# A recurrence's first step and the preparation of its second half, both ten half tiles later in the emission order

## The chip, the cores and the metric

One core of one Trainium2 chip runs the whole program. The metric is the device time of one execution in microseconds (us). The kernel before takes 2046.28 us, the median of three runs (2044.22 to 2046.51).

## The reference

A model with two blocks over 512 tokens of width 1024, all in float32. The first block has two layers. Each projects the modulated and normalised input `h` with one wide matrix, gives the pieces to three mixers (a causal pool mixer, a retention with 4 heads, an RWKV-7 time mix with 8 heads), gates the three results, merges them and projects back. The second block is attention and a mixture of 32 experts; the change does not touch it. The part that matters here is the time mix, in the reference a scan over the tokens:

```python
def step(S, inp):
    r_t, w_t, k_t, v_t, a_t, b_t = inp
    sa = jnp.einsum('bhvk,bhk->bhv', S, a_t)
    S = (S * w_t[:, :, None, :] + sa[..., None] * b_t[:, :, None, :]
         + v_t[..., None] * k_t[:, :, None, :])
    return S, jnp.einsum('bhvk,bhk->bhv', S, r_t)
```

## The kernel before

**Dense tiles.** The projections are cut into tiles of 128 output columns by 512 tokens. A tile is 24 matmuls of 128x512: 8 blocks of the inner width, each as three products of high and low parts (`mm3`, L313; the matmul itself is L354 without and L356 with a pin, see below). Its weights come by SyncE's queue (SP) into one of three buffers (`wst`, L297), ScalarE takes the high part (L307) and VectorE, or GpSimd for one tile in five, the low part (L310).

**Side work in half tiles.** After every half tile, `mm3` calls `tick` (L363), which takes generators of side work one step further: the recurrence (`rwkv`, L507), the retention's heads (`ret_heads`, L1045) and the pool mixer's groups (`pool_groups`, L931). With `RWKV_RATE = 1.0` the recurrence goes one `yield` per half tile. What they emit goes between the dense matmuls.

**Order on the engines.** A planner makes one fixed list for each engine before the program runs, by the order of emission and by its own costs of what is ready. On the chip each engine goes through its list in order. One thing is written by hand: each step of the recurrence sets `self.pin`, and `mm3` puts the next dense tile's first matmul behind that pin (`pinned`, L358). Dense work emitted after a step of the recurrence can therefore not run ahead of that step.

**The recurrence of a layer** goes over chunks of 64 tokens in two halves of four heads. `rwkv_prep` (L559, 19 yields) prepares a half: norms and decays (L571 to L628), the Gram matrices (L646, stored by L650), and then the inverses by forward substitution, 31 steps of two VectorE instructions each (L674 a product, L676 a sum), each needing the one before. Its result goes to memory (L682, L684). `rwkv_chain` (L688) is the recurrence itself: after `wait` empty yields it loads the first chunks' Gram matrices and inverses (`gt` L698, `ti` L700), and its first step is `inverse1`, whose matmul reads `ti`, then four steps per chunk. `rwkv` runs the preparation of the first half, then the chain of the first half beside the preparation of the second (through `late`, L515), then the chain of the second half, then the outputs (`rwkv_out`, L846).

**What runs beside it.** In half tiles from the start of the side work: 0 to 8 the retention's values, 8 to 20 the six tiles of the second half's r, k and v, 20 to 36 the eight q and k tiles of the retention, each turned by a rotary embedding (VectorE L1024, L1026 and L1027, then an add on GpSimd, L1028), 36 to 52 the pool mixer's eight tiles, 52 to 76 the first branch (gate tiles and branch tiles), 76 to 124 the second branch and the gates ahead of the third. At 124 `self.drain(rs)` (L1126) takes what is left of the recurrence. The first preparation ends at half tile 20, the first step of the chain comes at 26, and the second preparation begins at 21, since its tiles are there only then.

Of the kernel before, what the change touches and what calls it, by code (L numbers as in the profile page):

```python
# [179 lines left out]
class Layers:  # L180
# [326 lines left out]
    def rwkv(self, l, t, wa, out):  # L507
        prep = lambda hf: self.rwkv_prep(l, hf, t[hf][0:2], t[hf][2:4], t[hf][4:6], wa)
        ops = yield from prep(0)
        ys, nxt = yield from self.both(self.rwkv_chain(l, *ops, wait=CHAIN_WAIT), self.late(t, prep))  # L510
        (_, ys) = yield from self.both(self.rwkv_out(0, ys, ops[3]), self.rwkv_chain(l, *nxt))
        yield from self.rwkv_out(1, ys, nxt[3])
        out += ops[3] + nxt[3]

    def late(self, t, prep):  # L515
        while len(t) < 2:
            yield
        return (yield from prep(1))
# [1424 lines left out]
ATT_RATE = 4.0  # L1943
NEX = 5
NOH = 3
CHAIN_WAIT = 6


# [14 lines left out]
```

## Time and profile before

| | us |
|---|---|
| median of three runs | 2046.28 |
| the profiled execution | 2044.99 |
| its span, first to last instruction | 2043.2 |
| TensorE busy with matmuls | 1862.0 (91%) |
| VectorE busy | 1088.7 (53%) |
| ScalarE busy | 591.8 (29%) |
| GpSimd busy | 549.4 (27%) |
| mean granted TensorE clock, share of 2.4 GHz | 0.946 |

The first layer lies at about 60 to 740 us, the second at 740 to 1440 us, the second block behind them. A matmul's row overlaps the next one's, since matmuls are pipelined, so the distance between starts is what a matmul costs in a run of them. Of the 40 slices of the span (51 us each) TensorE is busy under 70% in four: the first, the fifth (204 to 255 us, 40 to 49%), the eighteenth (868 to 919 us, 60 to 69%) and the last. The fifth and the eighteenth lie one in each layer, at the same place of its work.

### The profile page before, as it was taken

The page shows a single profiled execution, that of the slowest core. Times are in us where ns is not written, and L with a number is a line of the kernel's source. Part 1 is how long each engine was busy: PE and PEld are TensorE (multiplying, and loading weights), DVE is VectorE, ACT ScalarE, POOL GpSimd, SP SyncE. Part 2 cuts the span into 40 slices and gives each one's busy share as a digit, 9 for nine tenths or more (in the row PEclk, how much of TensorE's full clock was granted, in tenths as well). Part 3 has the DMA queues.
Part 4 walks back from the last instruction along what each step waited for, and adds up shares of the span by engine and source line. Part 5 has one row for each costly group of instructions (what it writes and reads, how often), then busy time and mean ns, then how long its engine had stood idle before and what let it go on. Part 6 is the DMA issues. An engine that isn't in the chain of part 4 may idle for free. (4 is left out here: it accounts for less than half of the span.)

```text
span 2043.2 us, 26468 instructions
## 1 busy us (share of the span) xinstructions
PE 1862.0 (91%) x10178; PEld 1364.9 (67%) x10178; DVE 1088.7 (53%) x2285; ACT 591.8 (29%) x1086; POOL 549.4 (27%) x447
## 2 busy tenths in 40 slices
PE   6899498999999989967999999999999999899996
PEld 3777266777787868745667778777778768444443
DVE  4656779644533555495774243246554546344435
ACT  3332112332322333221233232234334334111112
POOL 1342244454566401232330122230110122100000
PEclk9999598999999989978899999999999969899998
DMA  7424143333343533312322323243422225799981
GB/s 296 134 90 117 30 119 87 97 122 118 108 145 108 172 102 93 119 47 60 109 67 88 92 66 93 83 118 118 168 73 78 73 109 217 312 424 416 403 347 42
DMA packets 103128, 289.03 MB, mean 141 GB/s; under 512 B 31112, under 2 KB 44296, under 8 KB 94808
## 3 DMA queue, kind: packets, MB, share of 16 engines
q1 hardware_dynamic: 97912, 267.40, 38.4%
q0 software_dynamic: 5088, 19.93, 2.6%
q8 instruction: 81, 1.33, 0.3%
q14 instruction: 47, 0.39, 0.1%
HBM read 268.90 MB, written 21.01 MB: 142 GB/s over the span
## 5 line engine op out<-in xcount | busy, mean ns | idle before, releaser
L354 PE MATMUL mm<-hi,wlo 128*128 128x512 f32 x1424 | 567.5, 399 | 2.0 <-DVE wlo L310 1.5
L354 PE MATMUL mm<-lo,whi 128*128 128x512 f32 x1424 | 567.0, 398 | 0.1
L354 PE MATMUL mm<-hi,whi 128*128 128x512 f32 x1296 | 519.3, 401 | 15.3 <-DVE rw L502 6.2
L307 ACT ACTIVATE whi<-wst 128x1024 fp32r<-128x1024 f32 (+1 forms) x202 | 193.0, 957 | 575.7 <-PE mm L354 390.1
L354 PEld LDWEIGHTS mm<-hi,wlo 128*128 128x128 f32 x1424 | 272.2, 191 | 69.6 <-issue 4.5
L354 PEld LDWEIGHTS mm<-lo,whi 128*128 128x128 f32 x1424 | 273.0, 192 | 63.7 <-issue 6.5
L354 PEld LDWEIGHTS mm<-hi,whi 128*128 128x128 f32 x1296 | 248.0, 192 | 77.8 <-ACT hi L486 7.8
L310 DVE TENSOR_TENSOR wlo<-wst,whi 128x1024 fp32r<-128x1024 f32 (+1 forms) x162 | 188.0, 1162 | 180.6 <-ACT whi L307 169.3
L310 POOL TENSOR_TENSOR wlo<-wst,whi 128x1024 fp32r<-128x1024 f32 (+1 forms) x40 | 87.5, 2188 | 279.7 <-ACT whi L307 279.6
L1802 PE MATMUL pp<-eg,xt 128*64 128x512 f32 x512 | 114.8, 601 | 0.2 <-PEq L1852 0.2
L437 POOL TENSOR_TENSOR wad<-wad,cact 128x1024 f32<-128x1024 f32 x32 | 65.3, 2040 | 180.2 <-DMA wad<-wada 150.7
L439 POOL TENSOR_TENSOR wad<-wad 128x512 f32<-128x512 f32 (+2 forms) x96 | 98.0, 1021 | 6.2
L1802 PEld LDWEIGHTS pp<-eg,xt 128*64 128x64 f32 x512 | 37.2, 139 | 74.7 <-issue 74.4
L354 PE MATMUL mm<-vhi,hi 128*128 128x256 f32 x256 | 75.3, 298 | 6.2 <-ACT vhi L970 4.0
L908 POOL TENSOR_TENSOR acc<-acc,tg 128x512 f32<-128x512 f32 x32 | 49.9, 1561 | 97.3 <-DVE tg L906 80.2
L354 PE MATMUL mm<-vlo,hi 128*128 128x256 f32 x256 | 74.9, 295 | 0.7 <-DVE vlo L971 0.6
L354 PE MATMUL mm<-vhi,lo 128*128 128x256 f32 x256 | 74.4, 292 | 0.0
L1842 PE MATMUL mm<-y,ohT 128*128 128x512 f32 x256 | 69.2, 409 | 3.2 <-DVE xr L1844 1.6
L1770 POOL DMA_INDIRECT xg<-hx,idx x16 | 15.5, 969 | 205.7 <-DVE xt L1793 151.0
L356 PE MATMUL mm<-hi,whi 128*128 128x512 f32 x128 | 65.5, 511 | 0.0
L674 DVE TENSOR_TENSOR tmp<-tt,lt 64x31 f32<-64x31 f32 (+15 forms) x124 | 58.2, 469 | 9.8 <-DMA lt<-gd 7.9
L1827 PE MATMUL ms<-ed,eht 128*64 128x512 f32 x256 | 58.7, 599 | 4.2 <-ACT eht L1817 4.0
(408 smaller groups left out, 2863.6 us busy)
## 6 DMA issues: line engine op xcount, KB each, us to landing
wst<-win SPq DMA_DIRECT2D x154, 512.0 KB, 3.7
eg<-egu SPq DMA_DIRECT2D x31, 2048.0 KB, 14.2
ed<-edn SPq DMA_DIRECT2D x31, 1024.0 KB, 10.2
wad<-wada SPq DMA_DIRECT2D x48, 512.0 KB, 4.2
wst<-wbr SPq DMA_DIRECT2D x48, 256.0 KB, 2.8
gd<-gs SPq DMA_DIRECT2D x64, 128.0 KB, 2.2
gt<-gd SPq DMA_DIRECT2D x32, 256.0 KB, 3.0
wst<-wout SPq DMA_DIRECT2D x16, 512.0 KB, 4.1
```

The costliest lines, as they stand in the source:

```text
L307: nc.scalar.activation(hi, w, AF.Copy)
L310: e.tensor_tensor(lo, w, hi.bitcast(F32), op=OP.subtract)
L354: return op(*args, **kw)
L356: return op(*args, **kw)
L437: nc.gpsimd.tensor_tensor(w, w, self.cact.unsqueeze(2).to_broadcast([128, 8, 128]), op=OP.mult)
L439: nc.gpsimd.tensor_add(w[:, :n], w[:, :n], w[:, n:2 * n])
L674: nc.vector.tensor_tensor(t, tt[:, 0:j + 1, j:j + 1].to_broadcast([2 * nu, j + 1, n]), lt[:, j:j + 1, j + 1:].to_broadcast([2 * nu, j + 1, ...
L908: nc.gpsimd.tensor_add(acc[d], acc[d], t)
L1770: self.last_row = self.nc.gpsimd.indirect_dma_start(xg, None, self.hx[:, :], bass.IndirectOffsetOnAxis(ap=idx, axis=0))
L1802: nc.tensor.matmul(p[64 * i:64 * i + 64], x[:, k, 64 * i:64 * i + 64], wts[e + i][0][:, k], start=k == 0, stop=k == 7)
L1827: nc.tensor.matmul(py[64 * i:64 * i + 64], ht[:, 128 * k + 64 * i:128 * k + 64 * i + 64], wts[e + i][1][:, k, 512 * c:512 * c + 512], star ...
L1842: nc.tensor.matmul(p, oT[:, 128 * tb:128 * tb + 128], y, start=i == 0, stop=i == len(parts) - 1)
```

## The change

Two constants. The chain of the first half waits 16 yields instead of 6 before its first loads, and the preparation of the second half lets 10 yields pass before it looks whether its tiles are there. Both are in each of the two layers.

```diff
     def late(self, t, prep):
+        for _ in range(PREP_WAIT):
+            yield
         while len(t) < 2:
             yield
         return (yield from prep(1))
...
-CHAIN_WAIT = 6
+CHAIN_WAIT = 16
+PREP_WAIT = 10
```

No instruction is added or taken away. In half tiles, the chain's first step goes from 26 to 36; the second preparation goes from 21 to 30, nine later, since one yield passed before with the tiles not there yet. The chain of the first half then ends at 69 instead of 59, that of the second at 103 instead of 93.

## Rows read from the trace of the kernel before

**Rows 1.** Stretches: start:end, length, busy PE, PEld, DVE, ACT, POOL, clock, DMA.

```profile
198.90:246.20 47.30, 14.17 (x46) 7.32 (x44) 37.31 (x71) 7.83 (x12) 15.91 (x13) 0.54 0.16 42
890.40:935.20 44.80, 15.89 (x57) 8.84 (x56) 34.88 (x73) 8.78 (x13) 13.00 (x9) 0.59 0.14 33
246.20:397.00 150.80, 135.89 (x915) 104.11 (x915) 115.85 (x257) 41.57 (x77) 66.03 (x53) 0.93 0.32 92
```

**Rows 2.** Waits of TensorE: waiter, what it waited for: total us, times, longest.

```profile
PE rm L354 <- DMA ti<-tn: 42.3, 2, 22.0
PE pp L356 <- DVE pbd L802: 14.1, 9, 4.4
```

**Rows 3.** Timeline, TensorE around the first step: start, us, engine, line, operation.

```profile
198.54 0.39 PE L354 MATMUL mm<-hi,wlo 128*128 128x512 f32 x1
...
244.24 0.28 PE L354 MATMUL rm<-ti,gt 32*32 32x32 f32 x2 [21.99 <-DMA ti<-tn]
...
246.16 0.78 PE L356 MATMUL mm<-hi,whi 128*128 128x512 f32 x1
...
890.02 0.39 PE L354 MATMUL mm<-hi,wlo 128*128 128x512 f32 x1
...
935.18 0.78 PE L356 MATMUL mm<-hi,whi 128*128 128x512 f32 x1
```

**Rows 4.** Timeline, the end of the substitution on VectorE and the store behind it.

```profile
236.99 0.20 DVE L676 TENSOR_TENSOR tt<-tt,tmp 64x31 f32<-64x31 f32 x1
...
237.22 0.93 SPq L684 DMA_DIRECT2D gd<-tt  x2
...
926.11 0.20 DVE L676 TENSOR_TENSOR tt<-tt,tmp 64x31 f32<-64x31 f32 x1
```

**Rows 5.** VectorE by line, 178.7 to 237.3: operation, count, busy us, mean ns, idle before.

```profile
L674 DVE TENSOR_TENSOR tmp<-tt,lt 64x31 f32<-64x31 f32 (+15 forms) x31 | 18.3, 592 | 4.3 <-DMA lt<-gd 3.9
L676 DVE TENSOR_TENSOR tt<-tt,tmp 64x31 f32<-64x31 f32 (+15 forms) x31 | 14.0, 452 | 0.6
L310 DVE TENSOR_TENSOR wlo<-wst,whi 128x1024 fp32r<-128x1024 f32 x3 | 3.6, 1213 | 0.0
L597 DVE TENSOR_TENSOR_SCAN cum<-rst,lw 128x512 f32<-128x512 f32 x2 | 2.4, 1216 | 0.0
L1026 DVE TENSOR_TENSOR ry<-mm,sin 64x512 f32<-64x512 f32 x3 | 2.1, 693 | 0.1
...
L278 DVE TENSOR_SCALAR ry<-rv 128x16 int32<-128x16 int32 x1 | 0.2, 159 | 0.0
```

**Rows 6.** The same by line in the second layer, 872.4 to 926.4.

```profile
L676 DVE TENSOR_TENSOR tt<-tt,tmp 64x31 f32<-64x31 f32 (+15 forms) x31 | 14.1, 455 | 0.6
L674 DVE TENSOR_TENSOR tmp<-tt,lt 64x31 f32<-64x31 f32 (+15 forms) x31 | 10.9, 353 | 2.7 <-DMA lt<-gd 2.3
L592 DVE TENSOR_SCALAR ag<-ag 128x512 f32<-128x512 f32 x2 | 3.0, 1484 | 0.0
...
L276 DVE TENSOR_SCALAR rv<-sn 128x16 f32<-128x16 f32 x1 | 0.2, 158 | 0.0
```

**Rows 7.** Timeline, two dense matmuls twenty apart in an undisturbed run.

```profile
184.65 0.39 PE L354 MATMUL mm<-lo,whi 128*128 128x512 f32 x1
...
189.19 0.39 PE L354 MATMUL mm<-hi,whi 128*128 128x512 f32 x1
```

**Rows 8.** Timeline, substitution products without and with GpSimd at work, and a rotary add.

```profile
191.15 2.63 POOL L1028 TENSOR_TENSOR rx<-rx,ry 128x512 f32<-128x512 f32 x1 [3.71 <-DVE ry L1027]
...
209.67 0.40 DVE L674 TENSOR_TENSOR tmp<-tt,lt 64x252 f32<-64x252 f32 x1
...
213.26 2.00 POOL L437 TENSOR_TENSOR wad<-wad,cact 128x1024 f32<-128x1024 f32 x1
213.54 2.00 DVE L674 TENSOR_TENSOR tmp<-tt,lt 64x256 f32<-64x256 f32 x1
```

**Rows 9.** Timeline, the recurrence's last output and the last gate ahead of `drain`.

```profile
569.81 0.86 DVE L859 SCALAR_TENSOR_TENSOR rw<-rm,hw,rw 128x128 f32<-128x128 f32 x3
...
638.60 0.58 ACT L890 ACTIVATE tg<-mm 128x512 f32<-128x512 f32 x1
```

## The prediction, before the changed kernel ran

> **What bounds the kernel now.** TensorE, busy for 91% of the span, so a change pays only where TensorE stands still. I read the waits of TensorE first: one line stands out, the matmul that reads `ti`, 42.3 us in two waits [rows 2]. It is the chain's first step, once in each layer. The timeline around it shows what it costs: the last dense matmul before it starts at 198.54, the step's own at 244.24, the next dense one, pinned behind it, at 246.16; in the second layer 890.02 and 935.18 [rows 3]. For 47.2 and 44.8 us no dense work starts. TensorE has 14.2 and 15.9 us of small matmuls in these stretches, at a granted clock of 0.54 and 0.59 [rows 1], so near its lower level of 1.2 GHz; at the full clock they would take some 7 to 8. About 40 and 37 us are lost.
>
> What the step waits for is VectorE: the last substitution sum starts at 236.99, its store goes out at 237.22 [rows 4], and the matmul follows 7.3 us after the sum. In the stretch VectorE is busy 37.3 of 47.3 us [rows 1], and the rest of the stretch is mostly this way through memory. So the hold is a backlog of VectorE: 62 dependent instructions of the first half's substitution, with other work let in between. By line, the substitution took 18.3 and 14.0 us, dense splits and rotary work about 10, and the second half's preparation 16.8 us, 34 instructions in 21 lines, of which the first and the last are shown [rows 5]; in the second layer it took 25.0 and 21.9 [rows 6].
>
> **The change part by part.**
>
> *The step moves back by ten half tiles.* A dense tile costs 24 matmuls of 0.227 us (4.54 us for twenty [rows 7]), 5.45 us. Five tiles, the last five of the retention's q and k, are 27.2 us of TensorE work that now comes ahead of the pin and fills the hold. This is the gain if the step opens when it does now.
>
> *What these five tiles put on VectorE.* They are rotary tiles. Five times three instructions of about 0.69 us [rows 5] are 10.3 us; the splits of four tiles at 1.21 us (every fifth is GpSimd's) are 4.8 us. About one retention head runs with them: some six full-width instructions and twelve small ones, by the nearest lines (0.69 and 0.16 us [rows 5]) 6 us. Sum 21 us, on the engine for which the step waits.
>
> *What they put on GpSimd.* Five rotary adds, up to 2.6 us each. Beside a GpSimd instruction of 2.00 us a substitution product took 2.00 us; one of nearly its size, with GpSimd idle, 0.40 [rows 8]. No row says how many of the five adds will meet a VectorE instruction; the bounds are 0 and 12 us. I take 5, since the loop of the first layer, which met most of this, is 7 us longer than that of the second [rows 5, 6].
>
> The Trainium skill's page "SBUF — State Buffer", section "Who interferes with whom", says that a VectorE instruction with two inputs in SBUF and a GpSimd instruction that reads SBUF exclude each other for the whole instruction. By it every add would hold VectorE in full, an estimate of 12 us in place of 5, and the sum below would come out 14 us higher; the row above shows one such case, while the mean of all 62 was 0.52 us ([rows 5]: 32.3 us by 62), near the undisturbed 0.40.
>
> *The second preparation moves back by nine.* Its 16.8 and 21.9 us were work let in between the substitution's instructions, and they leave to the extent that they now come behind it. They start 24.5 us of dense work later, while the hold stays, so some still get in. Bounds: all of it leaves, or none. I take three quarters, 12.6 and 16.4 us.
>
> *When the step opens.* First layer: 21 + 5 − 12.6 = 13.4 us later, so it saves 27.2 − 13.4 = 13.8 us. Second: 21 + 5 − 16.4 = 9.6 later, saves 17.6. TensorE is ready for the step at about 199 + 27 + 7 (small matmuls) = 233 and the step opens at about 258: I expect a wait on `ti` still, of 15 to 25 us in place of 22 plus the waits ahead of it.
>
> *The stage behind.* The preparation's work that filled the hold now lies behind it, beside the pool mixer and the first branch. There VectorE is busy 115.9 and TensorE 135.9 of 150.8 us [rows 1]; 12 to 16 us more still fit, but not always in time. Bounds 0 and 6 us in each layer; I take 2, since TensorE lost only 15 us in the whole stage while VectorE carried the other substitution.
>
> *What I cost at nothing.* The end of the recurrence moves ten half tiles back, 27 us; its last output is at 570 and the last gate ahead of `drain` at 639 [rows 9], so 69 us cover it. Were that cover gone, the third branch would wait for the difference. On SP the chain's `gt`, `ti` and `ca` loads and the preparation's stores are moved past five weight loads; a weight load held by a full buffer could hold them up by one tile, 5.5 us, but no wait for weights stands among TensorE's long ones. On GpSimd the preparation's multiplications now queue with the pool mixer's adds, priced in the stage behind. The chain and the preparation keep their distance but for one half tile, so the chain of the second half finds its inverses as early as now.
>
> *Sum.* −13.8 − 17.6 + 2 + 2 = −27.4 us. Against the profiled execution's 2044.99 (span 2043.2) this is 2017.6; that execution is 1.3 us under the median of three, within their spread. I predict 2018.
>
> **The rivals.**
>
> *The hold moves but hardly shrinks.* If the planner still lets most of the preparation in between, and GpSimd's adds hold VectorE in full, the step opens 21 + 12 = 33 us later in each layer, more than the 27.2 us that were filled in: up to 6 us lost per layer. With half of each it is about 21 + 8 − 9 = 20 us, a gain of 7. Time 2030 to 2050, middle 2038. For it speaks that VectorE was hardly idle before 237; against it that the preparation's emission is nine half tiles later and that priority goes by emission.
>
> *The hold vanishes.* If the substitution gets VectorE ahead of the rotary work, it ends where it does now or, with the preparation out, up to 17 us earlier, and the five tiles plus the small matmuls (34 us) cover most of the 47 and 45. Each layer saves 27 to 34 us: 1977 to 1991. Against it: the row order shows one other instruction between most substitution steps, and the five tiles offer just that.
>
> *Slower: the chain is starved in the pool mixer.* The first 16 half tiles of the chain now run beside the pool mixer's GpSimd adds, with the whole second preparation on VectorE. Each chunk hands over to VectorE some three times, and the dense tiles are pinned behind. Today such a wait (`pp` on `pbd`) costs TensorE 14.1 us in 9, the longest 4.4 us [rows 2]. At 1.5 us for each of 24 hand-overs in a layer it costs 36 us, 72 in both, against 31 saved: 2086; at 1.0 us 2062. It decides from 0.65 us per hand-over on. For it: the same preparation's substitution in the pool mixer was slow already. Against it: while that ran, TensorE lost 15 us in 151.
>
> *The change does not take.* The planner could bring preparation and step back to where they are ready. The pins speak against it, since dense work that is emitted before a pin is not held by it. Time 2045.
>
> **How the numbers follow.** The forecast (each layer saves 8 to 27 us, less the stage behind) 0.60, with its own range 1992 to 2033. The hold moves 0.18, about half of it faster. It vanishes 0.08. Slower by starved chain 0.12. No effect 0.02. A measurement of this kernel can tell some 0.2%, 4 us, from no change. Faster: 0.60 + 0.08 + 0.10 = 0.78; within: 0.06 + 0.02 = 0.08; slower: 0.02 + 0.12 = 0.14. The range has to leave out 0.2: most of the slower case (0.12) and most of the vanished hold (0.06); it goes from 1989 to 2044.
>
> **What would show it.** Right: the dense matmul behind the first step follows the last one ahead of it by 25 to 35 us in place of 47 and 45; five more rotary instructions stand ahead of the last substitution sum; that sum ends about 10 us later in time; the preparation's lines shrink between the substitution's. In the stage behind, TensorE's idle time grows by a few us only, and the recurrence's last output still comes well ahead of the last gate. Wrong: the wait on `ti` as long as before (the hold moved), gone (the hold vanished), or `pbd`, `q` and `uv` waits that add up to tens of us.

## The result, and the profile after

The changed kernel takes 2013.04 us (median of four runs, 2012.53 to 2017.36), the kernel before, run beside it, 2045.25 (2043.18 to 2046.51). The ratio is 0.9848, with an interval of 0.9831 to 0.9865: faster by 1.5%, some 31 us. The profiled execution took 2013.16, with a span of 2011.4, which is 31.8 less than before. The granted clock is 0.958 in place of 0.946.

Line numbers behind `late` are two higher than before: the substitution's product is L676 and its sum L678, the rotary multiplications L1026, L1028 and L1029.

Stretches of the kernel after: start:end, length, busy time of PE, PEld, DVE, ACT and POOL with instructions, granted clock, DMA share, GB/s. The first and the third begin where the stretches of [rows 1] began in the layer's work, to within a few matmuls, and end with the first step of the chain, which is five tiles further on. The second goes from there to the first gate.

```profile
197.70:263.80 66.10, 45.01 (x196) 33.81 (x195) 62.14 (x114) 16.18 (x22) 32.66 (x23) 0.84 0.27 82
263.80:370.20 106.40, 94.93 (x620) 72.18 (x619) 82.69 (x191) 29.28 (x53) 42.01 (x38) 0.89 0.32 88
875.50:936.70 61.20, 48.86 (x185) 34.18 (x184) 57.14 (x117) 15.64 (x20) 25.91 (x15) 0.83 0.23 59
```

Against [rows 1] TensorE's idle time fell from 33.1 (47.30 − 14.17) to 21.1 us (66.10 − 45.01) in the first layer and from 28.9 to 12.3 in the second: 12.0 + 16.6 = 28.6 us of the 31.8. Behind the step, up to the first gate, it fell from 14.9 (150.80 − 135.89) to 11.5 (106.40 − 94.93) in the first layer. Over the whole span TensorE's idle time fell by 26.1 us (181.2 to 155.1) and its busy time by 5.7 (1862.0 to 1856.3), for the same 10178 matmuls. VectorE is busy for 94 and 93% of the stretches up to the step; before it was 79 and 78%. The granted clock of these stretches rose from 0.54 and 0.59 to 0.84 and 0.83; dense work now runs between the small matmuls.

Waits of TensorE after (waiter, what it waited for: total us, times, longest):

```profile
PE qy L356 <- DVE pbd L804: 14.7, 12, 4.6
...
PE pp L356 <- DVE pbd L804: 8.9, 10, 1.7
PE mm L354 <- DVE ry L1029: 8.9, 6, 2.9
...
PE rm L354 <- DMA ti<-tn: 7.7, 1, 7.7
PE ms L1096 <- DVE sm L878: 6.8, 1, 6.8
```

The wait on `ti` fell from 42.3 in two [rows 2] to 7.7 in one. New lines took part of its place, and both kinds wait for VectorE: the retention's transposes (`sm`) and the dense tiles that need a rotary tile out of the way (`ry`). The two lines on `pbd` are 23.6 us together; before they were 14.1 [rows 2] and 6.3 (`PE qy L356 <- DVE pbd L802: 6.3, 8, 1.0`).

TensorE's timeline around the first step (start, us, engine, line, operation, wait before it), both layers:

```profile
213.17 0.39 PE L354 MATMUL mm<-hi,wlo 128*128 128x512 f32 x1
...
221.41 0.77 PE L354 MATMUL mm<-hi,whi 128*128 128x512 f32 x1 [1.80 <-DVE ry L1029]
...
228.47 0.39 PE L354 MATMUL mm<-hi,wlo 128*128 128x512 f32 x1
...
237.04 1.09 PE L1096 MATMUL ms<-ident,sm 128*128 128x128 f32 x4 [6.83 <-DVE sm L878]
...
244.36 0.50 PE L354 MATMUL mm<-hi,whi 128*128 128x512 f32 x1 [1.29 <-DVE ry L1029]
...
253.81 0.39 PE L354 MATMUL mm<-hi,wlo 128*128 128x512 f32 x1
...
261.89 0.31 PE L354 MATMUL rm<-ti,gt 32*32 32x32 f32 x2 [7.69 <-DMA ti<-tn]
...
263.84 0.78 PE L356 MATMUL mm<-hi,whi 128*128 128x512 f32 x1
...
907.36 0.39 PE L354 MATMUL mm<-hi,wlo 128*128 128x512 f32 x1
...
926.86 0.79 PE L354 MATMUL mm<-hi,whi 128*128 128x512 f32 x1 [0.78 <-DVE ry L1029]
...
934.77 0.24 PE L354 MATMUL rm<-ti,gt 32*32 32x32 f32 x2
```

Where one hold of 47 us stood [rows 3], there are three gaps without dense work: 213.17 to 221.41, 228.47 to 244.36 and 253.81 to 263.84, 34 us. Only the last is the step's. In the second layer the step waits for nothing; the longest gap there, 907.36 to 926.86, lies before it, and its first dense matmul waits for a rotary multiplication.

VectorE by line from 177.5 to 255, which answers to [rows 5] (operation, count, busy us, mean ns, idle before), and the last substitution sum from the timeline:

```profile
L678 DVE TENSOR_TENSOR tt<-tt,tmp 64x31 f32<-64x31 f32 (+15 forms) x31 | 17.4, 561 | 0.4
L676 DVE TENSOR_TENSOR tmp<-tt,lt 64x31 f32<-64x31 f32 (+15 forms) x31 | 12.3, 398 | 4.6 <-DMA lt<-gd 4.2
L310 DVE TENSOR_TENSOR wlo<-wst,whi 128x1024 fp32r<-128x1024 f32 x6 | 7.3, 1209 | 0.0
L1028 DVE TENSOR_TENSOR ry<-mm,sin 64x512 f32<-64x512 f32 x7 | 4.9, 693 | 0.1
...
L599 DVE TENSOR_TENSOR_SCAN cum<-rst,lw 128x512 f32<-128x512 f32 x2 | 2.4, 1210 | 0.0
...
L630 DVE TENSOR_TENSOR bk<-rw,di 128x512 f32<-128x512 f32 x1 | 0.7, 676 | 0.0
```

```profile
252.05 0.21 DVE L678 TENSOR_TENSOR tt<-tt,tmp 64x31 f32<-64x31 f32 x1
```

The loop now carries four more rotary tiles (7 for 3) and three more splits (6 for 3), and the last sum came at 252.05 instead of 236.99 [rows 4]. The preparation of the second half, though emitted nine half tiles later, is still there: L599, which is L597 of [rows 5], to L630, 34 instructions as before, all ahead of the last sum. In the second layer 30 of its 34 stand there, and two more rotary tiles and three more splits than before.

To see what the gain is at a later point of the work, the same gate and the same mark between the layers are taken in both traces. VectorE's and ScalarE's timelines, of before:

```profile
397.63 0.58 ACT L890 ACTIVATE tg<-mm 128x512 f32<-128x512 f32 x1
...
758.18 0.74 DVE L502 SCALAR_TENSOR_TENSOR rw<-mm,pv,rw 128x511 f32<-128x511 f32 x1
...
1366.99 0.58 ACT L890 ACTIVATE tg<-mm 128x512 f32<-128x512 f32 x1
```

and of after:

```profile
370.28 0.59 ACT L892 ACTIVATE tg<-mm 128x512 f32<-128x512 f32 x1
...
743.26 0.74 DVE L502 SCALAR_TENSOR_TENSOR rw<-mm,pv,rw 128x511 f32<-128x511 f32 x1
...
1335.33 0.58 ACT L892 ACTIVATE tg<-mm 128x512 f32<-128x512 f32 x1
```

At the first branch's first gate the changed kernel is 27.4 us ahead, at the end of the first layer 14.9, at the last gate of the second 31.7. So the layers saved 14.9 and 16.8. The 12 us between the first two numbers are no loss of speed: the chain is ten steps further back, so at that gate ten of its steps are still to be done. They come at the end of the recurrence, in the second branch, where with the chain beside it the gates follow each other by about 11.9 us, without it by 8.2 to 8.9. Ahead of these gates the lead is 29.6 us (525.28 − 495.71), behind them 14.8 (622.25 − 607.50).

### The profile page after: what moved, and what is told of

The parts are those of the page before. It is cut to its first block, busy times and chain, and to the rows that moved or that the text cites. A ratio compares the mean times of both kernels' runs of the same rounds, so it can differ in the third digit from the quotient of the medians.

```text
span 2011.4 us, 26483 instructions
## 1 busy us (share of the span) xinstructions
PE 1856.3 (92%) x10178; PEld 1363.6 (68%) x10178; DVE 1092.1 (54%) x2285; ACT 591.6 (29%) x1086; POOL 550.8 (27%) x447
## 5 line engine op out<-in xcount | busy, mean ns | idle before, releaser
L310 DVE TENSOR_TENSOR wlo<-wst,whi 128x1024 fp32r<-128x1024 f32 (+1 forms) x162 | 193.0, 1192 | 163.9 <-ACT whi L307 145.5
L356 PE MATMUL mm<-hi,whi 128*128 128x512 f32 x128 | 64.6, 505 | 0.0
L1844 PEld LDWEIGHTS mm<-y,ohT 128*128 128x128 f32 x256 | 44.8, 188 | 23.3 <-DVE xr L1846 13.0
```

What stands on the lines that cost most here:

```text
L310: e.tensor_tensor(lo, w, hi.bitcast(F32), op=OP.subtract)
L356: return op(*args, **kw)
L1844: nc.tensor.matmul(p, oT[:, 128 * tb:128 * tb + 128], y, start=i == 0, stop=i == len(parts) - 1)
```

## The experiments

Two theories stood at the start. **The backlog**: VectorE has a fixed amount of work before the step can open, and the preparation that is let in between is the part that the change defers. **The dry stretch**: in the kernel before VectorE itself stands still for a while in each layer. VectorE's timeline of before shows it:

```profile
251.13 0.69 DVE L1024 TENSOR_TENSOR rx<-mm,cos 128x512 f32<-128x512 f32 x1 [13.94 <-PE mm L354]
...
940.38 0.69 DVE L1024 TENSOR_TENSOR rx<-mm,cos 128x512 f32<-128x512 f32 x1 [14.06 <-PE mm L354]
```

In the first layer its last sum ends at 237.2, then come the way through memory, the step, and the first dense half tile behind the pin; only at 251.1 has VectorE work again. Of the 13.9 us between, 9 lie in TensorE's hold and 5 behind it. With five tiles ahead of the pin VectorE works through this time. In the kernel after its longest idle time around there is 3.6 us. A third theory is nearly the same thing seen from TensorE: five dense tiles now stand where it had none. The two differ in what more work on VectorE should cost, which the padded kernels below ask.

**The chain's wait alone.**

```diff
 CHAIN_WAIT = 16
-PREP_WAIT = 10
+PREP_WAIT = 0
```

> The first step at half tile 36, the second preparation at 21 as before the change. By the prediction's own term (the later preparation takes 12 to 16 us of VectorE work out of each layer's hold) this one loses that again: about 2040 us, and the last substitution sum of the first layer at about 265 us. By the theory read from the changed kernel's trace (all 34 instructions of the preparation still ran ahead of that sum, so the later emission moved nothing) the time is that of the changed kernel, 2013 us within 4, and the sum ends at about 252 us.

2016.03 us (2014.92 to 2018.05), ratio 0.9855 (0.9839 to 0.9872): within 3 us of the changed kernel. The step opens at 270.51 and 947.79, even later than there, and waits for no `ti`:

```profile
270.51 0.31 PE L354 MATMUL rm<-ti,gt 32*32 32x32 f32 x2 [0.91 <-DVE gs L648]
```

The last sum of the first layer came at 256.38, later than the 252 of the second theory and well before the 265 of the first. The long dry stretch is gone: VectorE's longest idle time around there is 6.3 us, a wait for a load ahead of the second substitution. The chain's wait carries nearly the whole gain.

**The preparation's wait alone.**

```diff
-CHAIN_WAIT = 16
+CHAIN_WAIT = 6
 PREP_WAIT = 10
```

> The first step at half tile 26 as before, the second preparation at 30. By the prediction's term the step opens 12 to 16 us earlier in each layer: about 2017 us, the wait on ti down to 5 to 10 us in each layer. By the theory that the later emission moves nothing: 2045 us within 4, and ti waits of about 42 us in two.

2047.12 us, ratio 1.0008 (0.9998 to 1.0017): no change. Yet it does what the backlog theory asks for. TensorE's timeline, and VectorE's behind it:

```profile
228.85 0.28 PE L354 MATMUL rm<-ti,gt 32*32 32x32 f32 x2 [26.64 <-DMA ti<-tn]
```

```profile
235.79 0.69 DVE L1026 TENSOR_TENSOR rx<-mm,cos 128x512 f32<-128x512 f32 x1 [14.13 <-PE mm L354]
```

The step opens 15.4 us earlier than at 244.24 [rows 3], and VectorE is busy 16.6 us less up to there (the windows below): here preparation work does leave the hold. But the dry stretch is as long as before, and most of the 15 us are given back: from the first branch's second gate on the lead is 3 us. Two pieces of work, the one up to the first dense matmul behind the step and the one from there to the same dense matmul in the first branch, first of this kernel, then of before:

```profile
180.00:230.80 50.80, 20.05 (x106) 16.42 (x104) 39.25 (x81) 5.71 (x7) 13.12 (x9) 0.71 0.25 70
230.80:418.00 187.20, 170.52 (x1091) 128.00 (x1089) 145.32 (x311) 54.02 (x98) 87.82 (x71) 0.92 0.31 91
```

```profile
180.00:246.20 66.20, 33.07 (x129) 21.44 (x128) 55.80 (x115) 12.77 (x17) 21.97 (x16) 0.67 0.20 54
246.20:420.92 174.72, 159.21 (x1059) 122.37 (x1057) 125.99 (x277) 47.84 (x88) 79.46 (x64) 0.94 0.33 98
```

The first piece lost 13.0 us of TensorE's busy time, most of it small matmuls, and 16.6 us of VectorE work, and the second took most of it up: 11.3 and 19.3 us more, at the same number of dense matmuls. Of the 15.4 us that the first piece is shorter, 12.5 came back in the second. Work that was done in the hold was done in time lost anyway; deferred, it takes time from dense tiles. Here an earlier step alone was no gain.

**The preparation forced behind the substitution.** The changed kernel, with the second half's first VectorE instructions issued behind the last substitution sum of the first half.

```diff
+    def behind(self, hf):
+        return self.tc.issue_after(self.last_tt.ins) if hf else nullcontext()
...
-        nc.vector.tensor_scalar(sn, st[:, :16], 1e-24, None, op0=OP.max)
+        with self.behind(hf):
+            nc.vector.tensor_scalar(sn, st[:, :16], 1e-24, None, op0=OP.max)
...
-            nc.vector.tensor_add(tt[:, 0:j + 1, j + 1:], tt[:, 0:j + 1, j + 1:], t)
+            self.last_tt = nc.vector.tensor_add(tt[:, 0:j + 1, j + 1:], tt[:, 0:j + 1, j + 1:], t)
```

(the scalings of `lw` and `ag` likewise)

> The changed kernel, with three VectorE operations of the second preparation (the maximum of its norms, and the scalings of its two sigmoids for each pair of heads) put behind the first half's last substitution sum in VectorE's order, so that the preparation really leaves the hold. If the hold's length counts by itself, the step opens about 15 us earlier in each layer and the time falls by 15 to 30 us, to 1983 to 1998. If the whole stretch is bound by VectorE (62 of 66 us busy in the first layer), the same work comes back behind the step: the sum ends 10 to 15 us earlier, but the time is 2005 to 2018.

2027.57 us, ratio 0.9907 (0.989 to 0.9924): 12 us slower than the changed kernel by the ratios, and outside both times that were expected. The last sum came 20 us earlier, at 231.87, but the step opened 9 us later, at 271.09. The top of TensorE's waits and the place:

```profile
PE rm L626 <- DVE ry L284: 20.2, 2, 12.5
PE mm L354 <- DVE ry L1035: 15.0, 6, 6.8
```

```profile
262.58 2.05 PE L626 MATMUL rm<-rw,blk 128*128 128x512 f32 x2 [12.53 <-DVE ry L284]
```

In TensorE's own list the preparation's matmuls still stood ahead of the step, and now they waited for VectorE work that had been put back. The test was meant to show what the preparation in the loop costs; what it shows is that a wait set on one engine can be paid on another whose list was not changed with it. What the step would give with both lists changed was not tried.

**The chain still further back.**

```diff
-CHAIN_WAIT = 16
+CHAIN_WAIT = 22
```

> The first step at half tile 42, three more dense tiles ahead of it, the second preparation at 30. The changed kernel still waits 7.7 us on ti in the first layer and not at all in the second. If that wait is what is left to fill, 4 to 8 us less: about 2007. If VectorE bounds the stretch and the chain's late end only moves, no gain: 2010 to 2020.

2002.76 us (1999.98 to 2008.07), ratio 0.979 (0.9765 to 0.9814), clock 0.964: faster than both kernels, 42 us below before, and a little better than expected. The step opens at 295.62 and 965.88 without a wait on `ti`. Between 197.7 and 290 TensorE is idle 18.5 us; in the changed kernel it is idle 23.7 us in the same time (92.30 − 68.62):

```profile
197.70:290.00 92.30, 73.81 (x348) 55.89 (x348) 84.31 (x155) 21.70 (x29) 44.66 (x33) 0.88 0.32 96
```

By the marks used above (the first layer's end at 739.57, the last gate at 1327.29) it is 3.7 us ahead of the changed kernel after the first layer and 8.0 at the end of the second. More than half of that comes in the second layer, where the changed kernel does not wait for `ti`; so that wait is not all that was left to win.

**Further still, in two ways.** Waits of 28 and 10, and of 28 and 22.

> The first step at half tile 28 + 20 = 48, the second preparation at 30. The run with 22 gained 10 us over the changed kernel where 4 to 8 was expected. If every half tile ahead of the step gives VectorE's backlog more cover, another 5 to 10 us: 1993 to 1998. If the backlog is covered by 22 already, 2000 to 2005. If the chain's end (109 + 6 = 115 of 124 half tiles) comes too late for the third branch, over 2005.

> The first step at 48, the second preparation at 42, the distance between the two as in the changed kernel. If the later preparation costs or gives nothing by itself, as the two single parts showed: the time of the run with 28 and 10, within 4 us. If it spreads VectorE's work over lighter stages: 5 to 10 us less than that run; if its end delays the second half's chain: more.

2008.47 us, ratio 0.9831 (0.9801 to 0.9861), and 2013.08, ratio 0.9863 (0.9834 to 0.9892). Neither improves on 22; the first is not told apart from it with certainty, since the intervals overlap. Putting the preparation back with the chain did not help here either.

**What VectorE's time costs, first attempt.** Fifteen sums over a constant, emitted in the first or the second half's substitution of the changed kernel; nothing reads their sums.

```diff
+            if hf == 0 and j % 2:
+                pad = self.S("pad", [128, 1], "pad", 1)
+                nc.vector.tensor_reduce(pad, self.rst, axis=AX.X, op=OP.add)
```

> The changed kernel with 15 more VectorE instructions in each layer, sums over a constant of 128x512 (0.67 us each by the nearest rows, 10 us a layer), one behind every second step of the first half's substitution. The theory that VectorE bounds the whole stretch, from the first substitution's start to the second one's end: 8 to 10 us more per layer, 2029 to 2034 us. The theory that the hold ahead of the first step is what counts: the same in this run, since the sum ends 10 us later; the next run tells the two apart. If TensorE bounds the stretch: 2013 to 2017.

> The same 15 instructions a layer, but behind the steps of the second half's substitution, which no pinned step waits for until a good 20 half tiles later. VectorE bounds the whole stretch: 2029 to 2034 us, as with the first half. Only the hold counts: 2011 to 2016.

2013.9 us, ratio 0.9848 (0.9814 to 0.9883), and 2014.6, ratio 0.9867 (0.984 to 0.9894). Nothing follows: the operand was ready from the beginning, the planner put the sums at the start of the program, and no substitution was padded; this is told here without a line of a trace.

**The same with a tie.** The sums read `tt`, so they can't leave the loop: fifteen of 64x512, 10.1 us in a layer. In the changed kernel's first substitution, then in its second, then both in the kernel before (`hf == 1` for the second).

```diff
+            if hf == 0 and j % 2:
+                pad = self.S("pad", [128, 16], "pad", 1)
+                nc.vector.tensor_reduce(pad[:2 * nu], tt[:, 0:16]..., axis=AX.X, op=OP.add)
```

> The padding of the two runs before read a constant, and the planner put it at the very start of the program, where it cost nothing; here each of the 15 sums a layer reads the inverse under construction (64x512, about 0.67 us), so that it has to run between two steps of the first half's substitution. VectorE bounds the stretch: 8 to 10 us a layer, 2029 to 2034 us. Only the wait for the first step counts: up to 10 us in the first layer, which waits on ti, and less in the second, which does not: 2015 to 2027. TensorE bounds it: 2011 to 2016.

> The same 15 sums tied into the second half's substitution. VectorE bounds the stretch up to that substitution's end: 2029 to 2034 us. VectorE has room there and only the chain's hand-overs feel it: 2013 to 2023.

> The kernel before with the same 15 sums tied into the second half's substitution. VectorE bounds the stage behind the hold: 16 to 20 us more, 2060 to 2065 us. It has room: 2043 to 2052. Beside the run on the changed kernel this tells whether the change made that stage more or less bound by VectorE.

> The kernel before with the 15 sums tied into the first half's substitution, the fourth of a two by two: on the changed kernel this cost 29 us, tied into the second half 2 us, and on the kernel before tied into the second half nothing. If the first substitution's end sets the first step in the kernel before as well, the hold grows by the padding's 10 us and what is let in between, 10 to 14 us a layer: 2062 to 2070 us. If VectorE's dry stretch behind the sum took up some of it, or work that now fits ahead of the step is missing later, less: 2048 to 2060.

| kernel | padded | us | ratio (interval) | cost by layer |
|---|---|---|---|---|
| after | first | 2042.23 | 0.9997 (0.9983 to 1.0011) | 15 us |
| after | second | 2014.74 | 0.987 (0.9835 to 0.9904) | not told from none |
| before | second | 2036.67 | 0.9973 (0.9953 to 0.9994) | none |
| before | first | 2054.12 | 1.0046 (1.0028 to 1.0064) | 4.7 us |

The cost is the difference of the ratios to the same kernel without pads, by 2044 us and two layers: (0.9997 − 0.9848) · 2044 / 2 = 15. Ten us of VectorE in the first substitution took the whole gain away. In the second substitution they cost nothing that can be told. The first layer's first substitution of the two kernels that are padded there by line, above the changed one, below the one before:

```profile
L676 DVE TENSOR_TENSOR tmp<-tt,lt 64x31 f32<-64x31 f32 (+15 forms) x31 | 15.5, 500 | 4.2 <-DMA lt<-gd 4.0
L678 DVE TENSOR_TENSOR tt<-tt,tmp 64x31 f32<-64x31 f32 (+15 forms) x31 | 14.2, 459 | 0.3
L681 DVE TENSOR_REDUCE pad<-tt 64x16 f32<-64x512 f32 x15 | 10.1, 675 | 0.1
L310 DVE TENSOR_TENSOR wlo<-wst,whi 128x1024 fp32r<-128x1024 f32 x7 | 8.5, 1211 | 0.5 <-ACT whi L307 0.5
```

```profile
L674 DVE TENSOR_TENSOR tmp<-tt,lt 64x31 f32<-64x31 f32 (+15 forms) x31 | 14.9, 481 | 4.6 <-DMA lt<-gd 4.3
L676 DVE TENSOR_TENSOR tt<-tt,tmp 64x31 f32<-64x31 f32 (+15 forms) x31 | 12.9, 416 | 0.6
L679 DVE TENSOR_REDUCE pad<-tt 64x16 f32<-64x512 f32 x15 | 10.1, 675 | 0.3
```

In the kernel before the substitution's own lines took 27.8 us here, 4.5 less than the 32.3 of [rows 5], so the pads added 5.6 us net; the last sum came 5.9 later (242.87), and 4.7 us a layer was the price: about one for one. In the changed kernel the lines took 29.7 us with and without pads, and the last sum came 21 us later (273.40), since another split and another rotary tile passed ahead of it. Up to the step, which opened 18.7 us later (280.62), VectorE had 12.7 us more to do and stood still for 6.0 us more (10.9 us for 5.0). Why ten us grew to 15 is explained by that only in part.

And the dry stretch stayed where the chain's wait stayed. VectorE's timeline of the padded kernel before:

```profile
257.05 0.69 DVE L1027 TENSOR_TENSOR rx<-mm,cos 128x512 f32<-128x512 f32 x1 [13.99 <-PE mm L354]
```

**What follows.** By the pads VectorE's work sets the pace in both kernels from the first substitution to the chain's first step: time added to it there is time lost. The change leaves that work as it is and gives VectorE dense tiles' work in the 14 us in which it stood still. In the four kernels in which the chain waits 6 or 16 yields, with either wait of the preparation, the 14 us stand in both that gain nothing and in neither of the two that gain; they sum to 28.0 us (13.94 + 14.06), TensorE's idle time fell by 28.6, and the gain is 31.8. That the one is the cause of the other fits the pads, but is not proved, since the dry stretch went only where the chain's wait moved and was never filled in another way; the wait of 22 gains 42 us, more than the dry stretches, so they are not all there is to win.

## Why the prediction was right, and where its steps were not

The time came out 5 us under the forecast, well inside the range, and by its mechanism in the main: five dense tiles ahead of the pin filled part of the hold, which shrank and was not merely moved. That the sum came so close is in part luck: it was made up of terms that missed in both directions.

*What bounds the kernel*: right about VectorE's backlog, but I read the hold as TensorE's loss only. VectorE, busy 37.3 of the hold's 47.3 us [rows 1], had 14 us with nothing to do from its last sum on, nine of them in the hold; I called the rest of the stretch "mostly this way through memory" and passed on. These two stretches are about as long as the gain. One figure there is off: at 0.59 [rows 1] the second layer's 15.9 us of small matmuls come to 9.4 at the full clock, not to 7 to 8, so some 35 us were lost there and not 37; the sum does not use it.

*The second preparation leaves the loop by three quarters* (12.6 and 16.4 us): this step failed. All 34 instructions ran ahead of the last sum in the first layer, 30 of 34 in the second. Emission is a priority only: the planner put this work between the substitution's dependent instructions all the same, though it was emitted nine half tiles later. In the run with the preparation's wait alone it did leave, where the dense tiles, and with them the splits and rotary work around the loop, were held back earlier; that this is why was not tried. And it was worth nothing even then: the step's opening is no measure of the gain where deferred work has to be done later.

*What the five tiles put on VectorE* (21 us): nearly right in kind; four more rotary tiles and three more splits passed ahead of the last sum in the first layer, two and three in the second, for five and four in the sum.

*GpSimd's hold on VectorE* (5 us, bounds 0 and 12; five adds of the 2.6 us named there would be 13, at the 2.4 us that three took in the mean in the first layer's loop they are 12): the substitution's 62 instructions took 29.7 us for 32.3 [rows 5] in the first layer and 29.5 for 25.0 [rows 6] in the second, with four more rotary adds in the first and two in the second: +1 us in the mean, near the lower bound, and less than the lines vary without such a cause (27.8 us in the kernel before with pads). The Trainium skill's page "SBUF — State Buffer", section "Who interferes with whom", has an exclusive lock for such pairs of instructions; the line sums here do not show the 12 us that the rule would give, while a single product of 2.00 us beside a GpSimd instruction of 2.00 [rows 8] does look like it. How often two meet was not counted.

*When the step opens* (13.4 and 9.6 us later): 17.7 us later in time (244.24 to 261.89), and 18.9 and 16.4 against dense work that started 1.2 and 14.9 us earlier. By my own way of counting the hold so saved 27.2 − 18.9 = 8.3 and 10.8 us, for 13.8 and 17.6 forecast. The term of the preparation alone would have taken off 12.6 and most of 16.4; fewer tiles' work ahead of the sum, and in the first layer less of GpSimd's hold, gave some of it back. The wait on `ti` was expected at 15 to 25 us in each layer; it was 7.7 and none, since TensorE itself came later, behind waits for VectorE (in the first layer 6.8 us for `sm`, 1.8 and 1.3 for `ry`).

*The stage behind* (2 us lost in each layer): by difference it won 6.6 and 6.0 (14.9 − 8.3 and 16.8 − 10.8), and TensorE's idle time up to the first gate fell by 3.4 us in the first layer. Small matmuls, and the preparation's VectorE work, were done ahead of the step and not behind it: of the 196 matmuls up to the step 112 are dense and 84 small, against 46 in all before [rows 1]; in the second layer 74 of 185 are small, against 57 in all. This term and the one above are the same work counted at two places, and so their misses nearly cancel: forecast −11.8 and −15.6, measured −14.9 and −16.8.

*Costed at nothing*: the end of the recurrence was hidden, as forecast. But the lead of 27 us at the first branch would have been misread as the gain; the chain's ten late steps take 12 of it back, and the text said nothing of where they are done.

*The rivals.* The hold that moves and hardly shrinks: no, idle time fell by 28.6 us, though its premise, that the preparation is let in, was right. The vanished hold: as one gap, yes, as lost time, no; 34 us in three gaps are left in the first layer. The starved chain: the waits on `pbd` rose by 3.2 us (20.4 to 23.6), not by 1 us for each of 24 hand-overs. No effect: no.

**Open** stays why the wait of 22 gains more than the dry stretches hold, why 28 does not gain more than 22, whether it is VectorE's dry stretches that the gain comes from, and how much of the preparation's share in the loop could be won, which would need TensorE's list and VectorE's to change together.

## What to carry to other kernels

Where a step holds back one engine's work, look at what the other engines do in the hold: the first place to look for time is the stretch in which the engine that sets the pace has itself run dry, and moving the step behind work for that engine fills it. Here that was 28 us for a gain of 32, and a longer wait won ten more that it does not explain. Work that is done in a hold costs little there, and deferring it to open the step earlier only moved the cost; read a gain at a point where the same work lies behind in both kernels. Emission order in a planned list is a priority and no promise, and whoever forces it on one engine must look at the lists of the others.

## What the runs showed of the hardware

Two things I had not expected. The granted clock of the stretch up to the step rose from 0.54 and 0.59 to 0.84 and 0.83. That is not only because the stretch now has dense tiles in it: in its long gaps too, where only small matmuls run, the clock did not fall as far as in the hold before.

```profile
228.80:244.30 15.50, 7.21 (x30) 5.51 (x29) 15.47 (x32) 5.13 (x8) 5.21 (x4) 0.67 0.23 68
907.75:926.80 19.05, 12.40 (x33) 6.59 (x33) 18.99 (x39) 7.05 (x9) 11.29 (x6) 0.68 0.23 49
```

What the clock gave was not measured by itself; the 5.7 us by which TensorE's busy time fell for the same matmuls hold it together with how far the matmuls overlap.

The other is how much the planner's order weighs. The product line of the substitution varied from 10.9 to 18.3 us for the same 31 instructions [rows 5, 6], and the kernel before with more work in its second substitution came out 0.27% faster (0.06 to 0.47%). That the order of the lists is the reason is likely, but no run took it by itself.
